# One transformer layer on one core: gate arithmetic over more half tiles, the norm before the FFN and the last 512 down columns by token tile, POOL's scale and shift behind the norm

## The chip, the core and the metric

The kernel runs on one core of a Trainium2 chip. The core has five engines that run at the same time and meet through semaphores: TensorE (PE) multiplies matrices, VectorE (DVE), ScalarE (ACT) and GpSimd (POOL) work element by element, SyncE (SP) starts transfers, which 16 DMA engines carry out. The metric is the device time of one execution in microseconds (us), the median of the runs; lower is better.

## The reference, cut to what matters

One layer over 256 tokens of 2048 features, all in float32. Every norm is over the 2048 features of a token.

```python
def _layer_norm(x, g, b):
    mu = mean(x, -1); var = mean(square(x - mu), -1)
    return (x - mu) * rsqrt(var + 1e-5) * g + b

def _conv_ffn(x, w_up, conv_w, conv_b, w_down):          # w_up 2048 x 11264, w_down 5632 x 2048
    gate, val = split(x @ w_up, 2, axis=-1)
    gate = _causal_dwconv(gate, conv_w, conv_b)          # 3 taps over the tokens
    return (gelu(gate) * val) @ w_down

x = _layer_norm(x, ln_in_g, ln_in_b)
x = _layer_norm(a * x + _hybrid_mixer(x, ...), ln1_g, ln1_b)                    # a = 2 ** 0.25
x = _layer_norm(a * x + _memory_cross_attention(x, mem, xq, xkv, xo), ln2_g, ln2_b)
x = _layer_norm(a * x + _conv_ffn(x, ffn_w_up, ...), ln3_g, ln3_b)              # the output
```

In the mixer, `_mlstm` takes a forget gate per head as `log_sigmoid(f_pre)`, sums it over the tokens, and keeps a running maximum of the input gate less that sum.

## The kernel before, in words

**Precision.** A float32 weight is cut in two parts that PE takes in its float32r format: `hi` (ACT casts it, L146) and `lo`, what is left (DVE subtracts, L147). Activations are cut the same way, into the two parts of a `parts` tile. A product is hi times hi, hi times lo and lo times hi: three matmuls.

**Weights.** `load_w` (L104) has SP fetch up to 1 MB of packed weights into one of three `raw` tiles (L112) and cuts it in two half tiles. Each half tile gets a `hi` and a `lo` buffer from `homes`: four buffers (`whl`), in the FFN three more (`whl2`). So ACT and DVE cut ahead of PE by as many half tiles as there are buffers.

**Two forms of product.** `cm_chunk` (L149) leaves channels on the partitions: 128 weight columns stand in PE, and the tokens move past, 512 columns where both parts move at once (L162), 256 for the first part against `lo` (L168). `tm_part` (L179) leaves tokens on the partitions: 128 tokens stand, and up to 512 weight columns move (L190), for both token tiles `tt` from one half tile. `tm_by_token` (L194) loads all half tiles first and then goes through token tile 0 and after it token tile 1 (L204). It is used for the last 256 of the 2048 columns of `xo` and of `down`.

**Order.** All engines take their instructions in order. The order on each engine is made when the program is built, by a scheduler that starts from the order of the code; `keep_in_program_order`, `issue_after` and the list `behind` (for the cuts of the coming half tiles) tie single instructions. Side work is written as a generator that `tick()` moves one `yield` forward after each half tile of the main stream.

**The gate job** (`gate_job`, L379). The twelve instructions of the log-sigmoid (L385 to L396) go on DVE, with an Exp and a Ln on ACT, in one piece. After one `yield` PE transposes the gates (L401, L402) and DVE makes the sums over the tokens (L406 to L410); four `yield`s later PE turns them back (L416).

**The norm before the FFN** (L744 to L758). After the last `xo` columns DVE adds the residual of a token tile (L648), takes its statistics (L652, L236), a few one-column instructions make the scale (`rsqrt`, L224 to L230, a Sqrt on ACT) and four instructions of 512 columns normalise it (L245). When both token tiles are through, `ln_transpose` takes blocks of 128 features: PE transposes (L254), ACT scales and shifts into `y` (L256), DVE rounds the first part (L258), and DVE or, for every second pair, POOL subtracts the second part (L259). Meanwhile `keep_warm(10)` gives PE ten matmuls whose results nobody reads (L84). `ln_affine` (L277) then lets POOL scale and shift `xt` itself for the residual, behind a small copy (`begun`).

**The FFN.** 44 chunks of `up` (each 128 gate and 128 value channels, L774) in four blocks of 11, and after each block the `down` columns (L789). In the last block the columns are 512, 512, 512, 256 and 256, the last by token (L786).

**The end.** Per token tile: residual and statistics of the last 256 columns, scale, then eight blocks of 128 tokens by 512 features: three by ACT and POOL (L806 to L808, `pooled`), five by DVE (L810, L811). Each goes out as 256 KB.

## Time and profile before

| | |
|---|---|
| median of 3 runs (lowest, highest) | 1542.41 us (1538.74, 1542.47) |
| the profiled execution: its own time, its span | 1544.83 us, 1542.8 us |
| PE, PEld busy | 98%, 85% of the span |
| DVE, ACT, POOL busy | 66%, 50%, 9% |
| mean granted clock of TensorE | 0.992 of full speed |
| moved by DMA | 292.87 MB, mean 190 GB/s |
| the chain of waits | PE 96%, DVE 2%, POOL 1%, ACT 1%, DMA 1% |

The span runs from the first to the last instruction; the execution's own time is 2.0 us longer. A row of the timeline gives the start, the length, the engine, the line of the kernel, the operation with its output and inputs, how many instructions were merged, and in brackets how long the engine sat idle before and what ended that. Matmuls overlap: how often one starts, not how long one lasts, tells what a stream of them costs. A plain float32 matmul leaves two records, a float32r matmul or a transpose one.

### The profile page before, as it was taken

The page shows a single profiled execution, that of the slowest core. Times are in us where ns is not written, and L with a number is a line of the kernel's source. Part 1 is how long each engine was busy: PE and PEld are TensorE (multiplying, and loading weights), DVE is VectorE, ACT ScalarE, POOL GpSimd, SP SyncE. Part 2 cuts the span into 40 slices and gives each one's busy share as a digit, 9 for nine tenths or more (in the row PEclk, how much of TensorE's full clock was granted, in tenths as well). Part 3 has the DMA queues.
Part 4 walks back from the last instruction along what each step waited for, and adds up shares of the span by engine and source line. Part 5 has one row for each costly group of instructions (what it writes and reads, how often), then busy time and mean ns, then how long its engine had stood idle before and what let it go on. Part 6 is the DMA issues. An engine that isn't in the chain of part 4 may idle for free.

```text
span 1542.8 us, 20558 instructions
## 1 busy us (share of the span) xinstructions
PE 1513.9 (98%) x8218; PEld 1318.0 (85%) x8218; DVE 1022.4 (66%) x1346; ACT 764.2 (50%) x987; POOL 142.6 (9%) x138
## 2 busy tenths in 40 slices
PE   8989999999999999999989999999999999999995
PEld 7988888888888888988878888888888888888885
DVE  6775999777776545664678765566655665566665
ACT  5554454586445445554355553455435554455541
POOL 1360000100006400000026000000000000000002
PEclk9999999999999999999999999999999999999998
DMA  9565555443655655444557555454554545545451
GB/s 344 173 210 194 189 196 179 171 174 134 255 204 198 219 191 191 141 152 151 192 189 240 198 198 203 177 207 169 203 202 171 212 168 198 207 168 215 160 195 55
DMA packets 46127, 292.87 MB, mean 190 GB/s; under 512 B 5392, under 2 KB 6032, under 8 KB 15312
## 3 DMA queue, kind: packets, MB, share of 16 engines
q1 hardware_dynamic: 43056, 282.64, 50.2%
q0 software_dynamic: 2544, 8.13, 2.6%
q8 instruction: 64, 1.05, 0.3%
q10 hardware_dynamic: 432, 0.79, 0.1%
q14 instruction: 31, 0.25, 0.0%
HBM read 289.44 MB, written 2.10 MB: 189 GB/s over the span
## 4 chain that ended last, share of the span: by engine, by line
PE 96%; DVE 2%; POOL 1%; ACT 1%; DMA 1%; SPq 0%; issue 0%; POOLq 0%; ACTq 0%
PE mm L190 37%; PE mm L162 35%; PE mm L168 19%; PE mm L204 1%; PE aux L693 1%; PE aux L723 1%; DMA raw<-wts_in 1%; POOL parts L259 1%; PE aux L254 0%; DVE xt L810 0%; ACT hi L146 0%; DVE lo L147 0%; PE aux L512 0%; PE aux L533 0%; ACT y L256 0%
## 5 line engine op out<-in xcount | busy, mean ns | idle before, releaser
L147 DVE TENSOR_TENSOR lo<-raw,hi 128x1024 fp32r<-128x1024 f32 (+4 forms) x536 | 645.5, 1226 | 358.9 <-ACT hi L146 280.0
L146 ACT CAST hi<-raw 128x1024 fp32r<-128x1024 f32 (+4 forms) x536 | 547.6, 1026 | 520.3 <-PE mm L190 270.4
L162 PE MATMUL mm<-parts,hi 128*128 128x512 f32 x2432 | 591.2, 393 | 2.7 <-POOL parts L259 2.7
L162 PEld LDWEIGHTS mm<-parts,hi 128*128 128x128 f32 x2432 | 446.8, 189 | 91.2 <-POOL parts L259 3.6
L168 PEld LDWEIGHTS mm<-parts,lo 128*128 128x128 f32 x2432 | 314.4, 191 | 13.6
L190 PE MATMUL mm<-hi,parts 128*128 128x512 f32 (+3 forms) x1088 | 318.0, 374 | 1.1 <-ACT hi L146 1.1
L168 PE MATMUL mm<-parts,lo 128*128 128x256 f32 x2432 | 318.8, 283 | 0.0
L190 PEld LDWEIGHTS mm<-hi,parts 128*128 128x128 f32 x1088 | 201.2, 190 | 34.5 <-ACT hi L146 2.0
L190 PE MATMUL mm<-hi,hp 128*128 128x512 f32 (+1 forms) x704 | 211.8, 382 | 0.0
L190 PE MATMUL mm<-lo,parts 128*128 128x512 f32 (+3 forms) x544 | 203.4, 374 | 1.2 <-DVE lo L147 1.2
L190 PEld LDWEIGHTS mm<-hi,hp 128*128 128x128 f32 x704 | 130.8, 188 | 25.7
L190 PE MATMUL mm<-lo,hp 128*128 128x512 f32 (+1 forms) x352 | 134.6, 383 | 0.0
L190 PEld LDWEIGHTS mm<-lo,parts 128*128 128x128 f32 x544 | 103.2, 190 | 18.3 <-DVE lo L147 2.6
L779 DVE SCALAR_TENSOR_TENSOR ac<-gv,pv,ac 128x255 f32<-128x255 f32 x88 | 50.1, 569 | 43.9 <-ACT ac L776 42.3
L172 ACT COPY gv<-mm 128x512 f32<-128x512 f32 x44 | 25.8, 586 | 103.9 <-PE mm L168 103.9
L190 PEld LDWEIGHTS mm<-lo,hp 128*128 128x128 f32 x352 | 66.2, 188 | 12.7
L807 POOL TENSOR_TENSOR xt<-xt,gb 128x512 f32<-128x512 f32 x3 | 4.5, 1496 | 677.5 <-ACT xt L806 677.5
L259 POOL TENSOR_TENSOR parts<-y,parts 128x512 fp32r<-128x512 f32 (+1 forms) x12 | 19.6, 1633 | 448.3 <-DVE parts L258 448.3
L451 DVE SCALAR_TENSOR_TENSOR cac<-cpad,pv,cac 128x256 f32<-128x256 f32 x120 | 51.3, 482 | 0.0
L287 POOL TENSOR_TENSOR xt<-xt,gb 128x512 f32<-128x512 f32 x24 | 41.6, 1752 | 43.6 <-DMA gb<-rows_in 36.6
L288 POOL TENSOR_TENSOR xt<-xt,gb 128x512 f32<-128x512 f32 x24 | 42.0, 1768 | 0.0
L781 DVE TENSOR_TENSOR ac<-gv,ac 128x256 f32<-128x256 f32 x44 | 19.2, 435 | 30.6 <-ACT ac L780 30.6
(227 smaller groups left out, 756.5 us busy)
## 6 DMA issues: line engine op xcount, KB each, us to landing
raw<-wts_in SPq DMA_DIRECT2D x238, 1024.0 KB, 4.9
raw<-wts_in SPq DMA_DIRECT2D x19, 768.0 KB, 4.3
gb<-rows_in POOLq DMA_DIRECT2D x24, 256.0 KB, 5.3
raw<-wts_in SPq DMA_DIRECT2D x4, 784.0 KB, 4.4
raw<-wts_in SPq DMA_DIRECT2D x6, 512.0 KB, 8.6
xt<-x_in SPq DMA_DIRECT2D x4, 512.0 KB, 9.7
raw<-memT_in SPq DMA_DIRECT2D x4, 512.0 KB, 3.6
gb<-rows_in SPq DMA_DIRECT2D x2, 1024.0 KB, 5.5
```

What stands on the lines that cost most here:

```text
L146: A.copy(hi, src)
L147: V.tensor_sub(lo, src, hi.bitcast(F32))
L162: nc.tensor.matmul(ps[:, j], lhsT=wH[:, kk, cs], rhs=a[:, k], start=(k == 0), stop=(k == KT - 1), skip_group_check=True)
L168: nc.tensor.matmul(ps[:, j, 0, :], lhsT=w[:, cs], rhs=a[:, k, 0, :], start=False, stop=(k == KT - 1), skip_group_check=True)
L172: A.copy(dst, ps[:, :, 1, :])
L190: nc.tensor.matmul(ps[tt][:, :n], lhsT=a[:, k, part, tsl], rhs=w[:, kk, :], start=(first and k == ks[0] and i == 0), stop=(last and k == k ...
L259: (G if k0 % 4 == 2 else V).tensor_sub(lo, y[:, 0:nk, :], hi.bitcast(F32))
L287: G.tensor_mul(sl, sl, gb[:, 0, :])
L288: G.tensor_add(sl, sl, gb[:, 1, :])
L451: tap = V.scalar_tensor_tensor(cac[:, i, :], cpad[:, i, j:j + S], pcol("ccw", i * CT + j), cac[:, i, :], ALU.mult, ALU.add)
L779: V.scalar_tensor_tensor(ac[:, o:], gv[:, 0, 0:S - o], pcol("fcw", f * 3 + t), ac[:, o:], ALU.mult, ALU.add)
L781: V.tensor_mul(ac, gv[:, 1, :], ac)
```

## The change

1. **Gates.** Seven `yield`s are put into the log-sigmoid's twelve instructions or behind them, and one between the sums over the tokens. The instructions are the same.
2. **Norm before the FFN.** The weights of the first `up` chunk are fetched and cut earlier, between the `xo` columns, into tiles of their own (`up0`, in the pool `pre`). `tm_by_token` calls `ln2_under` after each half tile, so the first token tile is normalised, transposed and cut (`ln_transpose_token`, four blocks of 128 features by 128 tokens at a time, always by DVE) beside the second token tile's matmuls. The first chunk is then multiplied by token tile (L829, L832 of the changed kernel): 64 matmuls of 2x128 columns and 64 of 128, where there were 32 of 512 and 32 of 256. `keep_warm` is gone. The second chunk's cuts are tied behind the norm's last ones, and POOL's copy `begun` reads the last part that the norm writes.
3. **Last down columns.** The last 512 columns (256 and 256) both go by token, the last 256 cut into a tile `wlast`. Each token tile is then closed whole: two residuals and statistics, scale, and all four blocks by DVE, written out by SP and ACT in turn. `pooled` is gone.

```diff
-    def load_w(mat, ks, cols):
+    def load_w(mat, ks, cols, into=None):
...
+            if into:
+                hi, lo = (t[:, k0 * n:k0 * n + sz] for t in into)
+            else:
...
+            after = behind.pop(0) if behind else []
...
+                with ExitStack() as order:
+                    for ins in after:
+                        order.enter_context(tc.issue_after(ins))
                     split(hi[:, o:e], lo[:, o:e], raw[:, k0 * n + o:k0 * n + e])
...
+    def cm_load(mat, c0, c1):
+        for g in range(0, KT, 8):
+            yield from load_w(mat, list(range(g, g + 8)), [(c0, c0 + P), (c1, c1 + P)])
...
+        for ks, wH, wL in loaded or cm_load(mat, c0, c1):
...
+        cm_close(ps, dst)
+    def cm_close(ps, dst, pinned=False):
+        copy = A.copy(dst, ps[:, :, 1, :])
+        if pinned:
+            tc.keep_in_program_order(copy)
...
-    def tm_by_token(a, mat, ks, cols, row0=0):
...
+    def tm_by_token(a, mat, ks, cols, row0=0, held=0, then=None):
+        store = act.tile([P, 2, 4096], F32R, name="wlast", tag="parts") if held else None
+        used, parts = 0, []
+        for c, col in enumerate(cols):
+            n = col[1] - col[0]
+            for g in range(0, len(ks), 8):
+                kg = [row0 + k for k in ks[g:g + 8]]
+                into = None
+                if c >= len(cols) - held:
+                    into = [store[:, i, used:used + len(kg) * n] for i in range(2)]
+                    used += len(kg) * n
+                parts += [(c, n, *p) for p in load_w(mat, kg, [col], into)]
+        ps = []
         for tt in range(NT):
-            for kl, wH, wL in parts:
+            ps.append(tm_open())
+            for pi, (c, n, kl, wH, wL) in enumerate(parts):
...
-                        nc.tensor.matmul(ps[tt][:, :n], lhsT=a[:, k, part, tt * P:(tt + 1) * P], rhs=w[:, kk, :],
+                        nc.tensor.matmul(ps[tt][c][:, :n], lhsT=a[:, k, part, tt * P:(tt + 1) * P], rhs=w[:, kk, :],
                                          start=(k == ks[0] and i == 0), stop=(k == ks[-1] and i == 2))
+                if then:
+                    then(ps, tt, pi)
         return ps
...
+    def ln_transpose_token(a, gname, bname, c, tt):
+        ps = aux.tile([P, 2, S], F32, name="aux").rearrange("p a (b t) -> p (a b) t", t=P)
+        y = yp.tile([P, 2, S], F32, name="y").rearrange("p a (b t) -> p (a b) t", t=P)
+        for k in range(4):
+            nc.tensor.transpose(ps[:, k, :], xt[:, tt, (4 * c + k) * P:(4 * c + k + 1) * P], ident)
+        for k in range(4):
+            made = A.activation(y[:, k, :], ps[:, k, :], AF.Identity, bias=pcol(bname, 4 * c + k), scale=pcol(gname, 4 * c + k))
+        hi, lo = (a[:, 4 * c:4 * c + 4, part, tt * P:(tt + 1) * P] for part in range(2))
+        V.tensor_copy(hi, y)
+        return made.ins, V.tensor_sub(lo, y, hi.bitcast(F32)).ins
...
-    def ln_affine(ri, rs):
-        tc.keep_in_program_order(G.tensor_copy(small.tile([P, NT], F32, name="begun"), rs))
+    def ln_affine(ri, begin):
+        tc.keep_in_program_order(G.tensor_copy(small.tile([P, NT], F32, name="begun"), begin))
...
             V.scalar_tensor_tensor(e, f, -1.0, f, ALU.mult, ALU.min)
+            yield
             A.activation(e, e, AF.Exp)
+            yield
             V.tensor_scalar_add(u, e, 1.0)
+            yield
             A.activation(w, u, AF.Ln)
             V.tensor_scalar_add(u, u, -1.0)
             V.tensor_scalar(z, u, 0.0, None, ALU.is_equal)
+            yield
             V.tensor_add(u, u, z)
             V.tensor_add(w, w, z)
+            yield
             V.reciprocal(u, u)
             V.tensor_mul(w, w, e)
+            yield
             V.tensor_mul(w, w, u)
             V.scalar_tensor_tensor(f, f, 0.0, w, ALU.min, ALU.subtract)
-            yield
+            for _ in range(3):
+                yield
...
             V.tensor_sub(g2, tg[0:4, 0:S], g1)
+            yield
             V.tensor_tensor_scan(mrow, g2, g2, 0.0, ALU.max, ALU.bypass)
...
-    for c in range(2, 4):
-        residual(tm_chunk(op, "xo", COLS_LAST[c]), c, COLS_LAST)
-    ps = tm_by_token(op, "xo", list(range(KT)), [COLS_LAST[4]])
-    xp = act_parts()
-    with keep_warm(10):
-        residual(ps, 4, COLS_LAST, tts=[0])
-        ln = ln_scales(len(COLS_LAST), [0])
-        for c in range(4):
-            ln_normalise(*ln, c, [0])
-        residual(ps, 4, COLS_LAST, tts=[1])
-        mv, rs = ln_scales(len(COLS_LAST), [1], ln)
-        for c in range(4):
-            norm = ln_normalise(mv, rs, c, [1])
-            first = norm if c == 0 else first
-            for k in range(4 * c, 4 * c + 4, 2 if c else 1):
-                ln_transpose(xp, "ln2_g", "ln2_b", k, 2 if c else 1)
-    ln_affine(4, rs)
+    with tc.tile_pool(name="pre", bufs=1) as pre:
+        up0 = [pre.tile([P, KT, 2 * P], F32R, name=n) for n in ("uph", "upl")]
+        for c in range(2, 4):
+            g = 8 * (c - 2)
+            into = [t[:, g:g + 8, :].rearrange("p k n -> p (k n)") for t in up0]
+            for _ in load_w("up", list(range(g, g + 8)), [(0, P), (DFF, DFF + P)], into):
+                pass
+            residual(tm_chunk(op, "xo", COLS_LAST[c]), c, COLS_LAST)
+        xp = act_parts()
+        ln, split0 = [], []
+        def ln2_norm(ps, tt):
+            with tc.issue_after(split0[1][1]) if tt else ExitStack():
+                residual([p[0] for p in ps], 4, COLS_LAST, tts=[tt])
+            ln.append(ln_scales(len(COLS_LAST), [tt], ln[-1] if ln else None))
+            for c in range(4):
+                ln_normalise(*ln[-1], c, [tt])
+        def ln2_under(ps, tt, pi):
+            if (tt, pi) == (0, 3):
+                ln2_norm(ps, 0)
+            if tt == 1 and pi >= 2:
+                for c in range(2 * pi - 4, 2 * pi - 2):
+                    split0.append(ln_transpose_token(xp, "ln2_g", "ln2_b", c, 0))
+        ps = tm_by_token(op, "xo", list(range(KT)), [COLS_LAST[4]], then=ln2_under)
+        ln2_norm(ps, 1)
+        ps0 = mm.tile([P, 2, 2, S], F32, name="mm")
+        for tt in range(NT):
+            tsl = slice(tt * P, (tt + 1) * P)
+            for g in range(0, KT, 4):
+                for i in range(2):
+                    for k in range(g, g + 4):
+                        for j in range(2):
+                            cs = slice(j * P, (j + 1) * P)
+                            if i == 0:
+                                nc.tensor.matmul(ps0[:, j, :, tsl], lhsT=up0[0][:, k, cs], rhs=xp[:, k, :, tsl], start=(k == 0),
+                                                 stop=(k == KT - 1), skip_group_check=True)
+                            else:
+                                nc.tensor.matmul(ps0[:, j, 0, tsl], lhsT=up0[1][:, k, cs], rhs=xp[:, k, 0, tsl], start=False,
+                                                 stop=(k == KT - 1), skip_group_check=True)
+                if tt == 0 and g >= 8:
+                    for c in range(g // 4 * 2 - 4, g // 4 * 2 - 2):
+                        split1 = ln_transpose_token(xp, "ln2_g", "ln2_b", c, 1)
+        behind.extend([[split0[3][0], split1[1]]] * 2 + [split1] * 2)
+        up1 = list(cm_load("up", P, DFF + P))
+    ln_affine(4, xp[:, KT - 1, 1, S - NT:S].bitcast(F32))
...
                 if f == 0:
-                    behind.extend([None] * 1 + [first.ins] * (4 - 1))
-                cm_chunk(xp, "up", f * P, DFF + f * P, gv)
+                    cm_close(ps0, gv, pinned=True)
+                else:
+                    cm_chunk(xp, "up", f * P, DFF + f * P, gv, up1 if f == 1 else None)
...
-            cols = COLS_LAST if final else COLS
-            for c in range(len(cols)):
...
+            if not final:
+                for c in range(4):
                     ps = tm_open()
-                    tm_part(ps, hp, "down", list(range(f1 - f0)), [cols[c]], row0=f0)
-                    residual(ps, c, cols, first=(bi == 0), last=final)
-    pooled = ((0, 0), (0, 1), (1, 0))
-    ln = None
-    nm = small.tile([P, NT], F32, name="nm")
+                    tm_part(ps, hp, "down", list(range(f1 - f0)), [COLS[c]], row0=f0)
+                    residual(ps, c, COLS, first=(bi == 0), last=False)
+            else:
+                for c in range(3):
+                    ps = tm_open()
+                    tm_part(ps, hp, "down", list(range(f1 - f0)), [COLS[c]], row0=f0)
+                    residual(ps, c, COLS_LAST, first=False)
+                last = tm_by_token(hp, "down", list(range(f1 - f0)), COLS_LAST[3:], row0=f0, held=1)
     for tt in range(NT):
-        residual(ps, 4, COLS_LAST, first=False, tts=[tt])
-        ln = ln_scales(len(COLS_LAST), [tt], ln)
-        mv, rs = ln
-        V.scalar_tensor_tensor(nm[:, tt:tt + 1], mv[:, tt, 0:1], -1.0, rs[:, tt:tt + 1], ALU.mult, ALU.mult)
-    for tt in range(NT):
+        for c in (3, 4):
+            n = COLS_LAST[c][1] - COLS_LAST[c][0]
+            sl = xt[:, tt, COLS_LAST[c][0]:COLS_LAST[c][1]]
+            tc.keep_in_program_order(V.tensor_add(sl, sl, last[tt][c - 3][:, 0:n]))
+            tc.keep_in_program_order(V.bn_stats(stats[:, tt, c, :], sl))
+        mv, rs = ln_scales(len(COLS_LAST), [tt])
         for c in range(4):
             cs = slice(c * 512, (c + 1) * 512)
             sl = xt[:, tt, cs]
-            if (tt, c) in pooled:
-                A.activation(sl, sl, AF.Identity, bias=nm[:, tt:tt + 1], scale=rs[:, tt:tt + 1])
-                G.tensor_mul(sl, sl, gb3[:, 0, cs])
-                G.tensor_add(sl, sl, gb3[:, 1, cs])
-            else:
-                V.scalar_tensor_tensor(sl, sl, mv[:, tt, 0:1], gb3[:, 0, cs], ALU.subtract, ALU.mult)
-                V.scalar_tensor_tensor(sl, sl, rs[:, tt:tt + 1], gb3[:, 1, cs], ALU.mult, ALU.add)
-                nc.sync.dma_start(out[tt * P:(tt + 1) * P, cs], sl)
-    for tt, c in pooled:
-        cs = slice(c * 512, (c + 1) * 512)
-        tc.keep_in_program_order(nc.scalar.dma_start(out[tt * P:(tt + 1) * P, cs], xt[:, tt, cs]))
+            tc.keep_in_program_order(V.scalar_tensor_tensor(sl, sl, mv[:, tt, 0:1], gb3[:, 0, cs], ALU.subtract, ALU.mult))
+            tc.keep_in_program_order(V.scalar_tensor_tensor(sl, sl, rs[:, tt:tt + 1], gb3[:, 1, cs], ALU.mult, ALU.add))
+            (nc.sync if c % 2 == 0 else nc.scalar).dma_start(out[tt * P:(tt + 1) * P, cs], sl)
```

Where instructions move, three places are shown, before and then changed.

PE at the gates, with token tiles of the gates `gm` transposed into `aux` between the matmuls of the value columns (`mm`). Before:

```order
L190 MATMUL mm<-lo,parts 128x384
L190 MATMUL mm<-hi,parts 128x384
L401 MATMUL aux<-ident,gm 128x128
L402 MATMUL aux<-ident,gm 128x128
L401 MATMUL aux<-ident,gm 128x128
L402 MATMUL aux<-ident,gm 128x128
L190 MATMUL mm<-hi,parts 128x384
L190 MATMUL mm<-lo,parts 128x384
```

Changed:

```order
L203 MATMUL mm<-lo,parts 128x256
L203 MATMUL mm<-hi,parts 128x256
L448 MATMUL aux<-ident,gm 128x128
L449 MATMUL aux<-ident,gm 128x128
L448 MATMUL aux<-ident,gm 128x128
L449 MATMUL aux<-ident,gm 128x128
L203 MATMUL mm<-hi,parts 128x256
L203 MATMUL mm<-lo,parts 128x256
```

The four transposes stand in the next group of columns now (256 wide, not 384): with 42 of 96 matmuls of the 384-wide group ahead of them before, and with all 96 of it and 72 of the next 96 now.

PE at the end of `xo` (`mm<-hi,parts`), the transposes of the norm (`aux<-ident,xt`) and the first `up` chunk (before `mm<-parts,hi`, now `uph` and `upl`). Before:

```order
L204 MATMUL mm<-hi,parts 128x256
L84 MATMUL aux<-ident 128x128 x10
L254 MATMUL aux<-ident,xt 128x128 x16
L162 MATMUL mm<-parts,hi 128x512 x3
L254 MATMUL aux<-ident,xt 128x128 x4
L162 MATMUL mm<-parts,hi 128x512 x4
L254 MATMUL aux<-ident,xt 128x128 x4
L162 MATMUL mm<-parts,hi 128x512 x2
L254 MATMUL aux<-ident,xt 128x128 x4
```

Changed:

```order
L230 MATMUL mm<-hi,parts 128x256
L294 MATMUL aux<-ident,xt 128x128 x8
L829 MATMUL mm<-parts,uph 128x2x128 x8
L832 MATMUL mm<-parts,upl 128x128 x8
L829 MATMUL mm<-parts,uph 128x2x128 x8
L832 MATMUL mm<-parts,upl 128x128 x8
L829 MATMUL mm<-parts,uph 128x2x128 x8
L832 MATMUL mm<-parts,upl 128x128 x8
L294 MATMUL aux<-ident,xt 128x128 x8
L829 MATMUL mm<-parts,uph 128x2x128 x8
```

The ten unread matmuls are gone. Eight transposes more stand 12 matmuls above the first row shown; the other 24 come in groups of eight, each group of the second token tile behind a part of the first tile's product.

DVE at the end, `xt` being the tokens, `mm` the last columns' sums. Before, from the middle of the first token tile's work:

```order
L811 SCALAR_TENSOR_TENSOR xt<-xt,rs,gb_6845 128x512
L650 TENSOR_TENSOR xt<-xt,mm 128x256
L811 SCALAR_TENSOR_TENSOR xt<-xt,rs,gb_6845 128x512
L652 BN_STATS stats<-xt 128x6
L236 BN_AGGR mv<-stats 128x2
L224 TENSOR_SCALAR ve<-mv 128x1
L810 SCALAR_TENSOR_TENSOR xt<-xt,mv,gb_6845 128x512
L226 RECIPROCAL rs<-nt 128x1
L810 SCALAR_TENSOR_TENSOR xt<-xt,mv,gb_6845 128x512
```

Changed, at the step from the first token tile to the second:

```order
L888 SCALAR_TENSOR_TENSOR xt<-xt,mv,gb_7009 128x512
L889 SCALAR_TENSOR_TENSOR xt<-xt,rs,gb_7009 128x512
L882 TENSOR_TENSOR xt<-xt,mm 128x256
L883 BN_STATS stats<-xt 128x6
L882 TENSOR_TENSOR xt<-xt,mm 128x256
L883 BN_STATS stats<-xt 128x6
L264 BN_AGGR mv<-stats 128x2
L252 TENSOR_SCALAR ve<-mv 128x1
L254 RECIPROCAL rs<-nt 128x1
```

Before, the two tiles' work is interleaved; now the second tile's residual stands behind all eight scalings of the first.

## Rows read from the trace of the kernel before

**Rows 1.** Waits of PE (who for whom: us in total, times, longest):
```profile
PE aux L401 <- DVE gm L396: 4.7, 1, 4.7
PE mm L162 <- POOL parts L259: 2.7, 2, 2.2
```

**Rows 2.** Timeline of PE at the gates (start us, us, engine, line, operation):
```profile
81.63 0.33 PE L190 MATMUL mm<-lo,parts 128*128 128x384 f32 x1
82.15 0.33 PE L190 MATMUL mm<-lo,parts 128*128 128x384 f32 x1
...
87.38 0.44 PE L401 MATMUL aux<-ident,gm 128*128 128x128 f32 x1 [4.72 <-DVE gm L396]
...
88.12 0.67 PE L190 MATMUL mm<-hi,parts 128*128 128x384 f32 x1
...
92.67 0.52 PE L190 MATMUL mm<-hi,parts 128*128 128x384 f32 x2
```

**Rows 3.** Windows at the gates: stretch, length, engines' busy (instructions), granted clock, DMA, GB/s:
```profile
88.10:92.70 4.60, 4.60 (x17) 4.60 (x16) 3.54 (x7) 0.83 (x1) 1.45 (x2) 0.52 0.54 114
```

**Rows 4.** Timeline of DVE at the gates:
```profile
87.07 0.17 DVE L396 SCALAR_TENSOR_TENSOR gm<-gm,gw 128x8 f32<-128x8 f32 x1
87.16 0.95 DVE L147 TENSOR_TENSOR lo<-raw,hi 128x768 fp32r<-128x768 f32 x1
```

**Rows 5.** Timeline of PE from the end of `xo` through three `up` chunks:
```profile
783.76 0.28 PE L204 MATMUL mm<-hi,parts 128*128 128x256 f32 x1
783.88 2.39 PE L84 MATMUL aux<-ident 128*128 128x128 f32 x20
...
794.81 0.73 PE L162 MATMUL mm<-parts,hi 128*128 128x512 f32 x2 [2.19 <-POOL parts L259]
...
819.46 7.44 PE L162 MATMUL mm<-parts,hi 128*128 128x512 f32 x32
826.74 4.00 PE L168 MATMUL mm<-parts,lo 128*128 128x256 f32 x32
830.57 1.78 PE L162 MATMUL mm<-parts,hi 128*128 128x512 f32 x7
```

**Rows 6.** Pieces of the chain of waits (start us, us, what):
```profile
97.72 0.98 PE aux L416 x8
...
772.52 10.09 PE mm L204 x84
```

**Rows 7.** Groups of instructions by line, shapes apart (count, busy us, mean ns):
```profile
L512 PE MATMUL aux<-qk 128*128 128x256 f32 x16 | 4.8, 380 | 0.0
L511 PE MATMUL aux<-qk 128*128 128x128 f32 x16 | 3.1, 275 | 0.0
L568 ACT ACTIVATE dm<-dm,atok 128x128 f32<-128x128 f32 x4 | 1.5, 386 | 0.0
L259 DVE TENSOR_TENSOR parts<-y,parts 128x512 fp32r<-128x512 f32 x11 | 7.6, 692 | 0.3
```

**Rows 8.** Timeline of DVE, first token tile of the norm before the FFN:
```profile
778.32 0.42 DVE L648 SCALAR_TENSOR_TENSOR xt<-xt,mm 128x256 f32<-128x256 f32 x1 [3.15 <-PE mm L204]
778.78 0.43 DVE L652 BATCH_NORM_STATS2 stats<-xt 128x6 f32<-128x256 f32 x1
...
780.87 1.92 DVE L245 TENSOR_SCALAR xt<-xt,mv,rs 128x512 f32<-128x512 f32 x4
```

**Rows 9.** Timeline of ACT in `xo`'s fourth group of columns:
```profile
766.80 1.05 ACT L146 CAST hi<-raw 128x1024 fp32r<-128x1024 f32 x1 [1.83 <-PE mm L190]
```

**Rows 10.** Timeline of the end, all engines:
```profile
1518.76 0.76 DVE L650 TENSOR_TENSOR xt<-xt,mm 128x256 f32<-128x256 f32 x2 [3.64 <-PE mm L190]
...
1524.04 1.40 DVE L810 SCALAR_TENSOR_TENSOR xt<-xt,mv,gb 128x512 f32<-128x512 f32 x2
...
1526.36 0.28 PE L204 MATMUL mm<-hi,hp 128*128 128x256 f32 x1
...
1537.53 1.59 POOL L808 TENSOR_TENSOR xt<-xt,gb 128x512 f32<-128x512 f32 x1
```

43 lines of the change are left out of this document (16 added, 27 removed).

## The prediction

> **What bounds the kernel now.** First the page's shares: PE is busy 98% of the span and makes up 96% of the chain of waits, so time is won where PE stands still or works without need, and nowhere else. The list of PE's waits comes next, and it is short: 4.7 us once for the gates on DVE, 2.7 us for POOL in the norm before the FFN [rows 1]. These waits are less than what the two places cost, because work around them is stretched too. So the third view is PE's timeline there: the reader is to compare the time between two points with what the same matmuls take elsewhere. The fourth place stands in no list of PE's waits, since PE has finished: from its last matmul at 1526.36 to the end of the span at 1542.8 are 16.4 us, in which DVE, ACT and POOL close the output [rows 10]. I treat the change as these three places and price each by its own rows.
>
> **Gates.** PE stands 4.72 us before the first transpose of the gates [rows 2]. After it PE runs at a granted clock of 0.52 on average, which is the 1.2 GHz level for nearly all of the stretch [rows 3]. That stretch holds 17 matmul records; two are the last transposes and one starts at its end, so 14 matmuls of 384 columns start between 88.12 and 92.67, 4.55 us. At the usual pace of 0.52 us for three [rows 2] they take 2.43 us: 2.1 us lost to the clock. The four transposes take 0.74 us from 87.38 to 88.12, where 0.12 each is usual (below): 0.3 us lost. Together 7.1 us.
>
> The new yields do not move DVE's arithmetic: in the built order its twelve instructions stay in one piece at the same place. What moves are the transposes, from behind 42 of this group's 96 matmuls to behind all of them and 72 of the next group's. PE so goes on past 82.5, and what is late next is the `lo` cut of the seventh half tile of 12 matmuls, which stands on DVE right behind the arithmetic and ends at 87.16 + 0.95 = 88.1 [rows 4]. PE reaches it after 6 matmuls of the fourth half tile and 24 of the next two, 30 x 0.173 = 5.2 us, at 87.7. I take 0.4 us for this wait, so 6.7 us won. With no wait of several microseconds the clock should not fall. ACT loads its table once more, for an Exp that comes between two Sigmoids, beside PE's work; DVE's sums over the tokens have more than two half tiles until PE asks for them.
>
> **Norm before the FFN.** From 783.88, where `xo` is done, two chunks of `up` and 32 transposes fill PE to 819.46: 35.6 us [rows 5]. One chunk in the steady run behind it takes from 819.46 to 830.57, 11.1 us [rows 5]. A 128x128 pass takes 0.12 us: the ten unread matmuls are 20 records in 2.39 us [rows 5]. So 2 x 11.1 + 32 x 0.117 = 26.0 us are needed and 9.6 us are lost: the unread matmuls, the waits, and the slow clock after them.
>
> The change starts the first token tile's norm 5.8 us earlier, beside the second tile's `xo` matmuls. Its price is PE work: the first chunk by token has 64 pairs of a matmul of 2x128 columns and one of 128. The 256-column matmuls of `xo` come every 0.12 us (84 in 10.09 us) [rows 6]; I take that for the 2x128 ones. A float32r matmul of 128 columns is not in the trace. From below, half of a 256-column one, 0.06 us, if the columns alone counted. From above, the plain float32 price: two passes of 0.117 for 128 columns, and for 256 columns two of 0.117 + 0.105 (380 less 275 ns [rows 7]), 0.44 us. The nearest row is the turning back of the gates: only four columns move, on 128 columns of weights, and one still comes every 0.98 / 8 = 0.12 us [rows 6], so the weights set the pace there. I take 0.12: 64 x 0.24 = 15.4 us, 4.3 more than the chunk before.
>
> The Trainium skill (TensorE: Matmul & The Clock Gate, "LDWEIGHTS") has a load take its columns over 1.2 per nanosecond, 107 ns for 128, whatever the rows; by that rule halving the columns of the moving side gains nothing, and the four-column row agrees. The same page ("Back-to-back issue gap") gives about 81 ns per matmul of 128 columns in a stream; the sum by that is an estimate of 5.2 us for the 64 narrow ones in place of 7.7, so 2.5 us more won, which no row here shows.
>
> Does the norm keep up? Count from 778.2, the first token tile's last matmul. DVE takes 2.55 us from the residual to the first normalised block and 0.48 per block [rows 8], so blocks stand at 3.1, 3.6, 4.1, 4.6. The first eight transposes stand 12 matmuls from the end, at 4.3: no wait. Each block of 128 features by 4 costs ACT 4 x 0.39 [rows 7] and DVE twice at most 0.69 [rows 7]: parts ready at about 7.5, 9, 10.5, 12. PE is through `xo` and its transposes at 7.6 and needs 1.9 us per quarter of a token tile's product, so the parts just keep ahead. DVE does the second tile's residual in between, from about 8.5, and normalises it by about 13 to 14.5; PE asks for it at 13.4. I take 0.5 us of waits in all. 9.6 - 4.3 - 0.5 = 4.8 us won. The earlier cut of the first chunk's weights (four more casts and subtractions in the `xo` columns) costs nothing as long as cutting waits for PE and not for the weights, as it does there [rows 9]; if it did not, four times 1.2 us on DVE would show. The second chunk's `lo` cuts wait behind the norm, but its first 32 matmuls, 7.3 us, need only `hi`. POOL starts some microseconds earlier than before, with the FFN's first residual far off.
>
> **The end.** A token tile's last matmul now comes after 66 instead of 33 of them. The first tile is complete where DVE begins the fourth group's residual today, 1518.76 [rows 10]. It takes one residual and statistics more (2 x 0.46), the same 2.55 us to the scale [rows 8], and eight scalings, 0.67 each where POOL is quiet (two end 1.40 after the first starts [rows 10]): 3.5 + 5.4 = 8.9, until 1527.6. PE's last matmul has ended by then (1526.6), so the second tile starts 1 us late and ends at 1536.5. Before, the last operation is POOL's, ending at 1539.12 [rows 10], 3.7 us ahead of the span's end, and what follows it is one output of 256 KB, as now. 2.6 us won. Cutting the last 256 columns into `wlast` waits for no buffer, so PE should not see it.
>
> **Sum.** 6.7 + 4.8 + 2.6 = 14.1 us, from 1544.8 us of the profiled execution to 1530.7. The median shown is 2.4 us below that execution, and so the forecast is 1542.4 - 14.1 = 1528.3, given as 1528.
>
> **Rivals.**
> *Narrow ones dear.* Only the 128-column matmuls cost the plain float32 price: 64 x (0.12 + 0.234) = 22.7, 11.6 more than before. 9.6 - 11.6 - 0.5 = -2.5 there, 6.8 in all: 1535.6. For it: plain float32 does pay two passes [rows 5]. Against: the operands stay float32r, and 256 columns of them run at a quarter of the plain price.
> *Both dear, and slower.* Moving the tokens in two pieces of 128 makes both kinds run at the plain price, PE being where it bites: 64 x (0.444 + 0.234) = 43.4, 32.3 more. 9.6 - 32.3 + 9.3 = -13.4: 1555.8. It decides from a pair at 0.47 us on, about twice what I take. Nothing in the trace speaks for it but that no row shows pieces.
> *The norm is late again.* ACT now has 32 instructions for 16, and the second tile's normalising stands behind the first's cuts on DVE; if each block came 1.2 us later, the 4.8 us go to waits, with a slow clock behind them: 1533.
> *The gates' wait only changes its name.* DVE's arithmetic is where it was, so if cuts behind it come as late as the transposes did, some 5 of 6.7 us stay: 1533.5. This is also the case in which the change does not do what it says. Against: PE has 30 matmuls ready that do not need the cuts.
> *Narrow ones cheap.* 0.06 us each saves 3.8 us on PE, of which the norm's pace gives back about 1: 1525.5.
>
> **How the numbers follow.** Forecast 0.52, narrow dear 0.14, both dear 0.07, norm late 0.13, gates 0.05, narrow cheap 0.09. The forecast's own range is 1524.5 to 1532, from the waits that I put at 0.4 to 1 us each. The range asked for goes from the cheap case to beyond the dear one: 1523 to 1538; outside it lie both dear and the tails of the others. What a measurement of this kernel can tell from no change is 0.3%, 4.6 us: faster is below 1537.8, slower above 1547. The dear, late and gates cases end mostly below it. Faster 0.86, same 0.07, slower 0.07.
>
> **What would show it.** Gates: no wait of PE at the transposes, a clock near 1 after them, and at most half a microsecond before the seventh half tile. Norm: the two matmuls of L829 and L832 both every 0.12 us, the second chunk done some 31 us after the last `xo` matmul, no wait for POOL. End: no POOL rows, the first token tile's scalings starting at about 3.5 us after its last matmul, and 13.5 to 14 us from the last matmul to the end. It is wrong if L832 costs over 0.2 us each, if PE waits for `lo` in the `xo` columns, or if the granted clock falls between the transposes.

## The result and the profile after

| | before | after |
|---|---|---|
| median (lowest to highest) | 1542.44 us (1538.74 to 1543.65) | 1530.07 us (1529.48 to 1530.86) |
| ratio after / before | | 0.9919, 95% interval 0.9906 to 0.9932 |
| the profiled execution: own time, span | 1544.83, 1542.8 us | 1529.72, 1527.8 us |
| PE busy, POOL busy | 98%, 9% | 99%, 9% |
| mean granted clock of TensorE | 0.992 | 0.996 |

The medians are 12.4 us apart, the profiled executions 15.1. The forecast was 1528 us: the time is 2 us longer, inside the range.

The list of PE's waits after (who for whom: us in total, times, longest) no longer has the two entries of [rows 1]:

```profile
PE aux L84 <- POOL ident L76: 1.6, 1, 1.6
PE mm L203 <- ACT hi L151: 1.4, 3, 0.8
PE mm L203 <- DVE lo L152: 1.4, 4, 0.8
PE mm L170 <- DVE gv L186: 0.3, 1, 0.3
```

What is left is the start of the program (up to 15.5 us), 0.16 us at the gates (below) and 0.3 us in the FFN.

**Gates.** The timeline of PE after, where [rows 2] had the wait of 4.72 us:

```profile
87.63 0.44 PE L203 MATMUL mm<-lo,parts 128*128 128x384 f32 x1 [0.16 <-DVE lo L152]
...
100.38 0.27 PE L448 MATMUL aux<-ident,gm 128*128 128x128 f32 x1
100.49 0.27 PE L449 MATMUL aux<-ident,gm 128*128 128x128 f32 x1
```

and the same window as in [rows 3] (the eighth field is the granted clock):

```profile
88.10:92.70 4.60, 4.60 (x31) 4.60 (x30) 4.36 (x4) 2.09 (x3) 2.33 (x2) 1.00 0.94 178
```

The transposes wait for nothing and come every 0.11 us, the clock is 1.00 where it was 0.52, and 31 matmul records lie in the window where 17 did, the last 8 of them with 256 columns in place of 384. DVE's arithmetic, in the timeline of DVE, stands where it stood [rows 4], still with 1.2 us for 8 elements:

```profile
82.26 1.26 DVE L432 TENSOR_SCALAR gu<-gu 128x8 f32<-128x8 f32 x1
83.55 1.22 DVE L433 TENSOR_SCALAR gz<-gu 128x8 f32<-128x8 f32 x1
84.81 1.21 DVE L435 TENSOR_TENSOR gu<-gu,gz 128x8 f32<-128x8 f32 x1
...
86.53 0.17 DVE L442 SCALAR_TENSOR_TENSOR gm<-gm,gw 128x8 f32<-128x8 f32 x1
```

**Norm.** The timeline of PE after, answering [rows 5], from the last transposes of the first token tile on:

```profile
777.11 1.04 PE L294 MATMUL aux<-ident,xt 128*128 128x128 f32 x8
778.19 1.21 PE L829 MATMUL mm<-parts,uph 128*128 128x256 f32 x8
779.24 1.00 PE L832 MATMUL mm<-parts,upl 128*128 128x128 f32 x8
780.08 1.16 PE L829 MATMUL mm<-parts,uph 128*128 128x256 f32 x8
...
794.86 7.50 PE L170 MATMUL mm<-parts,hi 128*128 128x512 f32 x32
802.20 4.00 PE L176 MATMUL mm<-parts,lo 128*128 128x256 f32 x32
806.03 1.30 PE L170 MATMUL mm<-parts,hi 128*128 128x512 f32 x5
```

Eight L832 start within 780.08 - 779.24 = 0.84 us, 0.105 each; eight of both take 1.83 to 1.89 us, 0.23 to 0.24 a pair. The second chunk is done 28.9 us after 777.11; eight transposes (1 us) already lie in front of that, so 29.9 us answer to the 35.6 of before.

**End.** The timeline of all engines after, answering [rows 10]:

```profile
1506.61 0.42 DVE L882 TENSOR_TENSOR xt<-xt,mm 128x256 f32<-128x256 f32 x1 [5.36 <-PE mm L230]
...
1509.82 0.74 DVE L888 SCALAR_TENSOR_TENSOR xt<-xt,mv,gb 128x512 f32<-128x512 f32 x1
...
1510.36 4.05 PE L230 MATMUL mm<-wlast,hp 128*128 128x256 f32 x33
...
1515.61 0.42 DVE L882 TENSOR_TENSOR xt<-xt,mm 128x256 f32<-128x256 f32 x1
...
1523.94 0.75 DVE L889 SCALAR_TENSOR_TENSOR xt<-xt,rs,gb 128x512 f32<-128x512 f32 x1
```

The scalings begin 3.2 us after the residual, and the second token tile starts 1.2 us after PE's last matmul ends (1514.4). That matmul starts at 1510.36 + 32 x 0.12 = 1514.2, so 13.6 us to the end of the span, where 16.4 were.

### The profile page after: what moved, and what is told of

Read it like the earlier page. It is cut to its first block, busy times and chain, and to the rows that moved or that the text cites. A ratio compares the mean times of both kernels' runs of the same rounds, so it can differ in the third digit from the quotient of the medians.

```text
span 1527.8 us, 20640 instructions
## 1 busy us (share of the span) xinstructions
PE 1509.6 (99%) x8262; PEld 1314.8 (86%) x8262; DVE 1022.2 (67%) x1350; ACT 764.2 (50%) x1001; POOL 131.3 (9%) x128
## 4 chain that ended last, share of the span: by engine, by line
PE 95%; DVE 3%; DMA 1%; ACT 1%; issue 0%; SPq 0%; POOL 0%; DVEq 0%; ACTq 0%
PE mm L170 36%; PE mm L203 35%; PE mm L176 18%; PE mm L230 1%; DMA raw<-wts_in 1%; DVE lo L152 1%; PE aux L741 1%; PE aux L771 1%; PE mm L829 1%; PE mm L832 0%; DVE xt L889 0%; DVE xt L888 0%; PE aux L282 0%; ACT hi L151 0%; PE aux L560 0%
## 5 line engine op out<-in xcount | busy, mean ns | idle before, releaser
L152 DVE TENSOR_TENSOR lo<-raw,hi 128x1024 fp32r<-128x1024 f32 (+3 forms) x528 | 639.7, 1235 | 336.2 <-ACT hi L151 260.8
L151 ACT CAST hi<-raw 128x1024 fp32r<-128x1024 f32 (+3 forms) x528 | 539.4, 1026 | 493.3 <-PE mm L203 250.9
L170 PE MATMUL mm<-parts,hi 128*128 128x512 f32 x2400 | 582.4, 393 | 0.3 <-DVE gv L186 0.3
L170 PEld LDWEIGHTS mm<-parts,hi 128*128 128x128 f32 x2400 | 440.6, 188 | 87.3 <-issue 0.7
L176 PE MATMUL mm<-parts,lo 128*128 128x256 f32 x2400 | 312.4, 282 | 0.0
L203 PE MATMUL mm<-hi,hp 128*128 128x512 f32 x660 | 205.9, 392 | 0.0
L203 PEld LDWEIGHTS mm<-hi,hp 128*128 128x128 f32 x660 | 124.1, 188 | 26.6
L203 PE MATMUL mm<-lo,hp 128*128 128x512 f32 x330 | 128.6, 390 | 0.0
L858 ACT ACTIVATE ac<-gv,pv 128x256 f32<-128x256 f32 x44 | 26.3, 599 | 26.8 <-DVE gv L186 26.8
L152 DVE TENSOR_TENSOR hp<-ac,hp 128x256 fp32r<-128x256 f32 x44 | 18.7, 426 | 21.5 <-ACT hp L151 21.5
```

Source lines behind the costliest of these rows:

```text
L151: A.copy(hi, src)
L152: V.tensor_sub(lo, src, hi.bitcast(F32))
L170: nc.tensor.matmul(ps[:, j], lhsT=wH[:, kk, cs], rhs=a[:, k], start=(k == 0), stop=(k == KT - 1), skip_group_check=True)
L176: nc.tensor.matmul(ps[:, j, 0, :], lhsT=w[:, cs], rhs=a[:, k, 0, :], start=False, stop=(k == KT - 1), skip_group_check=True)
L203: nc.tensor.matmul(ps[tt][:, :n], lhsT=a[:, k, part, tsl], rhs=w[:, kk, :], start=(first and k == ks[0] and i == 0), stop=(last and k == k ...
L858: A.activation(ac, gv[:, 0, :], AF.Identity, bias=pcol("fcb", f), scale=pcol("fcw", f * 3 + 2))
```

## The experiments

Each was timed against the kernel before in later rounds. "Changed" is the changed kernel with its 1530.07 us from above; e5, e10 and e11 build on one another. In the later rounds the kernel before has medians of 1543.55 to 1543.72 us, 1.1 to 1.3 above the 1542.44 of the result, and the changed kernel was not timed again. So the medians do not resolve a difference of about a microsecond to it.

| kernel | median (lowest to highest), us | ratio to before, interval |
|---|---|---|
| e1, gates back | 1537.00 (1535.31 to 1537.75) | 0.9961 (0.9947 to 0.9974) |
| e2, norm back | 1534.58 (1534.35 to 1534.91) | 0.9947 (0.9934 to 0.9959) |
| e3, end back | 1531.48 (1530.82 to 1532.38) | 0.9926 (0.9914 to 0.9939) |
| e4, narrow ones twice | 1537.89 (1537.45 to 1538.16) | 0.9967 (0.9955 to 0.9979) |
| e5, 64 bytes unused | 1528.55 (1528.02 to 1529.97) | 0.9902 (0.9887 to 0.9918) |
| e6, all at multiples of 128 | 1531.35 (1528.08 to 1532.31) | 0.9918 (0.9904 to 0.9932) |
| e7, gates back, fill | 1534.64 (1532.63 to 1534.86) | 0.9941 (0.9928 to 0.9953) |
| e8, chunk whole | 1534.27 (1533.79 to 1534.65) | 0.9940 (0.9928 to 0.9953) |
| e9, gates back, POOL later | 1529.61 (1529.12 to 1530.74) | 0.9911 (0.9894 to 0.9927) |
| e10, e5 and end early | 1528.86 (1528.23 to 1530.03) | 0.9908 (0.9893 to 0.9922) |
| e11, e10 and POOL later | 1527.29 (1526.09 to 1528.31) | 0.9896 (0.9882 to 0.9911) |
| e12, weight buffers back | 1532.07 (1529.91 to 1533.63) | 0.9925 (0.9912 to 0.9939) |

**One part undone (e1 to e3).** The hunks of the diff are taken back one at a time, as e1 does (it takes out eight `yield`s in or behind the log-sigmoid's instructions, for the change puts in eight there and not seven, and the one between the sums):

```diff
             A.activation(e, e, AF.Exp)
-            yield
             V.tensor_scalar_add(u, e, 1.0)
-            yield
...
-            for _ in range(3):
-                yield
+            yield
```

> The changed kernel with the gate job of the kernel before (no new yields); all else stays. Theory: the gates are worth what their place cost in the trace before, some 7 us (4.7 of waiting, 2.1 of slow clock, 0.3 of slow transposes), so 1530.1 + 7 = 1537 us, and PE again waits 4 to 5 us for DVE before the gate transposes, with a granted clock near 0.5 behind them. Rival: part of the gain only came from the neighbours (the cuts of the next half tiles late in either order): under 4 us slower, 1534 or less. Second rival: the gates explain the whole 7.6 us that the changed kernel is ahead at the last xo matmul of the first token tile, and a little more: 1538 or above.

> The changed kernel with the norm before the FFN and the first up chunk as they were before (both token tiles normalised, ten unread matmuls, 512 and 256 columns moving, POOL in the norm). Theory from the two traces: from the first token tile's last xo matmul to the end of the second up chunk 35.5 us where it was 41.3, so 5.8 us slower: 1535.9 us. Forecast's term: 4.8, so 1534.9. Rival: the FFN behind it, where the changed kernel took 692.5 us against 691.0, pays for the new order of buffers; then 1.5 us come back and the net is 4.3: 1534.4, with down groups of 512 columns again every 14.95 us rather than 15.1.

> The changed kernel with the last down columns and the output as they were before (512, 512, 512, 256, and only the last 256 by token tile; three blocks by ACT and POOL). Theory from the two traces: 16.4 us from PE's last matmul to the end in place of 13.5, so 2.9 us slower: 1533.0 us (forecast's term 2.6: 1532.7). Rival: taking the last 512 columns by token costs PE time that the tail hides in the comparison (cuts of 256 columns, a second buffer): then under 1.5 us slower.

Measured: 6.9, 4.5 and 1.4 us slower than changed, 12.8 in all, against 12.4 for the whole change: the parts add up. The spans of the profiled executions give 5.6, 4.9 and 1.8 us. e1 agrees with its theory. e2 agrees with the forecast's term; its rival has about the same size, but the rival's sign did not come (the down groups take 15.09 us, not 14.95). In e3 the rival's size came out, but not for the rival's reason. Its tail is as long as before (last matmul at 1513.19, span's end 1529.6: 16.4 us), so the new end is worth 2.8 us there. But PE comes to its last matmul 0.9 us earlier than in the changed kernel (there 1514.12), and the difference begins long before the end. The FFN's first residuals in e3, timeline of DVE:

```profile
921.58 1.29 DVE L696 SCALAR_TENSOR_TENSOR xt<-xt,mm 128x512 f32<-128x512 f32 x2
936.53 1.29 DVE L696 SCALAR_TENSOR_TENSOR xt<-xt,mm 128x512 f32<-128x512 f32 x2
```

and in the changed kernel, with the same order of instructions up to there:

```profile
921.75 1.29 DVE L696 SCALAR_TENSOR_TENSOR xt<-xt,mm 128x512 f32<-128x512 f32 x2
936.83 1.29 DVE L696 SCALAR_TENSOR_TENSOR xt<-xt,mm 128x512 f32<-128x512 f32 x2
```

A down group of 66 matmuls of 512 columns takes 14.95 us in one and 15.08 in the other. Before, too, it is 14.95; in e1, e2 and e4, with the new end, about 15.1.

**What 64 bytes do (e5, e6, e12).** The new end needs no tile `nm`. As the programs are built, `hp` and the FFN's own weight buffers so lie 64 bytes lower per partition: 96 above a multiple of 128, where they were 32 above one.

```diff
+    nc.vector.memset(small.tile([P, 8], F32, name="spare"), 0.0)     # e5 (two buffers: 64 bytes)
+    nc.vector.memset(const.tile([P, 24], F32, name="spare_c"), 0.0)  # e6, besides
+        ff1.tile([P, 16], F32, name="spare")                         # e12, alone
```

> The changed kernel with 64 bytes per partition left unused ahead of the FFN's tiles. Reason: the new end needs no nm tile, so hp and the three hi and lo buffers of the FFN lie 64 bytes lower than in the kernel before, and in all four kernels with the new end the down groups of 512 columns come every 15.1 us, in the two with the old end every 14.96, while up chunks are 0.2 % faster. Theory (the address): down groups every 14.96 us again, last PE matmul about 1 us earlier, 1529.2 us. Rival (something else in the new end, such as the tile wlast or its transfers): 15.1 us still, 1530.1.

> As the kernel with 64 bytes unused, and 96 more ahead of every large tile, so that the raw, hi, lo, parts and hp tiles all begin at a multiple of 128 bytes (before: 32 above one). If the place within 128 bytes sets the pace of the matmuls, up chunks and down groups change from 11.1 and 14.96 us by up to 1 % in either direction (1516 to 1542 us over the whole); if only the distance between hp and the weight buffers counts, which is the same as with 64 bytes, nothing changes against that kernel: 1529.2 us.

> The changed kernel with 64 bytes left unused between hp and the FFN's weight buffers: hp stays where the change put it (96 above a multiple of 128 bytes), the three hi and lo buffers of the FFN go back to 32 above one, as in the kernel before. If the place of the weight buffers sets the pace, down groups come every 14.96 us again as with 64 bytes ahead of both, 1529 us; if the place of hp does, 15.1 us as in the changed kernel, 1530.1 us; between the two, both count. Up chunks, which do not use hp, tell the weight buffers' part by themselves: 136.3 us between the fourth down group of a block and the first of the next where they lie as before, 136.06 as in the changed kernel.

In e5 the down groups come every 14.95 us again (timeline of DVE):

```profile
922.94 1.28 DVE L697 SCALAR_TENSOR_TENSOR xt<-xt,mm 128x512 f32<-128x512 f32 x2
937.89 1.28 DVE L697 SCALAR_TENSOR_TENSOR xt<-xt,mm 128x512 f32<-128x512 f32 x2
```

In e12, with `hp` where the change put it, every 15.10:

```profile
923.51 1.29 DVE L696 SCALAR_TENSOR_TENSOR xt<-xt,mm 128x512 f32<-128x512 f32 x2
938.61 1.28 DVE L696 SCALAR_TENSOR_TENSOR xt<-xt,mm 128x512 f32<-128x512 f32 x2
```

So the place of `hp`, which stands in PE in these matmuls, sets their pace. The weight buffers act on the up chunks, the other way. From a block's last down group to the next block's first there are eleven chunks and one down group. This takes 136.06, 136.28 and 136.12 us in the changed kernel, 136.34 each time in e5 and 136.49 in e12. The first of these stretches, timeline of DVE, in the changed kernel,

```profile
967.80 1.28 DVE L696 SCALAR_TENSOR_TENSOR xt<-xt,mm 128x512 f32<-128x512 f32 x2
...
1103.86 1.29 DVE L698 TENSOR_TENSOR xt<-xt,mm 128x512 f32<-128x512 f32 x2
```

and in e12:

```profile
969.61 1.28 DVE L696 SCALAR_TENSOR_TENSOR xt<-xt,mm 128x512 f32<-128x512 f32 x2
...
1106.10 1.29 DVE L698 TENSOR_TENSOR xt<-xt,mm 128x512 f32<-128x512 f32 x2
```

Less the down group, the eleven chunks take 121.0 to 121.2 us in the changed kernel and 121.4 in both others. e6 has 14.95 as well: `hp` at 0 or 32 above a multiple of 128 is fast, at 96 slow. Its distance to the FFN's own weight buffers is the same in the changed kernel as in e5, so that is not what counts; whether its place itself does or its distance to a tile that did not move, these kernels don't tell apart. In the trace e5 wins 0.8 us between its first down group and the last but one (561.14 us in place of 561.94); the medians say 1.5. The mechanism stays open, and `hp` put back with the weight buffers left low was not tried.

The medians of e6 and e12 miss their forecasts by 2 us, and the traces show where the profiled executions lose it. From the start of the second chunk to the first residual, the profiled executions take 126.9 us in the changed kernel, 128.3 in e5, 128.7 in e12 and 130.2 in e6. In that stretch PE's wait for `gv` goes from 0.3 us (changed) to 1.8 (e6), although each engine has the same instructions in the same order around it (790 to 860 us). There POOL scales and shifts for the FFN's residual, and a `lo` cut of 128x1024 takes DVE up to 2.3 us beside it, 1.22 later in the FFN; how many cuts are hit differs among the profiled executions. So the 64 bytes are to be read from the pace of the loops, not from medians a microsecond or two apart.

**The narrow matmul (e4).**

```diff
+                                for _ in range(2):
                                     nc.tensor.matmul(ps0[:, j, 0, tsl], lhsT=up0[1][:, k, cs], ...
```

> The changed kernel with each of the 64 matmuls of 128 columns of the first up chunk (weights upl) issued twice, so the lo product of that chunk is counted twice. Their price by itself. Theory: the load of the weights sets the pace, a little over 0.1 us each as the trace of the changed kernel has it (8 of them in 0.84 us), 64 x 0.105 = 6.7 us more where PE sets the pace there: 1536.8 us. If columns alone counted (0.06 us): 3.8 more, 1533.9. If they paid the plain float32 price (0.234): 15 more, 1545. If the norm and not PE set the pace in the first half of the chunk, up to half of it would vanish in waits: 1533.5 with waits of PE for DVE gone.

7.8 us slower, 0.12 for each of the 64; in the trace the second chunk starts 7.3 us later (802.17), 0.11 for each. The timeline of PE in e4:

```profile
779.64 1.90 PE L833 MATMUL mm<-parts,upl 128*128 128x128 f32 x16
781.38 1.15 PE L829 MATMUL mm<-parts,uph 128*128 128x256 f32 x8
```

16 in 1.74 us, 0.109 each: PE sets the pace, and half the columns save little. 0.06 and 0.234 are both excluded. The Trainium skill (TensorE: Matmul & The Clock Gate, "LDWEIGHTS") has 107 ns for loading 128 columns, which these rows bear out; the 81 ns of its "Back-to-back issue gap" no run here reaches.

**Token by token, or whole (e8).** The loop over `tt` around the first chunk is gone, and all transposes stand in front:

```diff
-        for tt in range(NT):
-            tsl = slice(tt * P, (tt + 1) * P)
+        for c in range(4):
+            split1 = ln_transpose_token(xp, "ln2_g", "ln2_b", c, 1)
```

> The changed kernel with the first token tile's norm as early as it is, but the first up chunk multiplied for both token tiles at once (32 matmuls of 512 columns and 32 of 256), behind all transposes. Theory: the split by token is what lets PE work under the second tile's norm; without it PE waits from the end of xo (777 us) until the second tile's first four blocks are cut (about 787), needs 11.1 us from there, plus 1 to 3 us of slow clock: the second chunk is done 4 to 7 us later, 1535 us. Rival: the split's 64 narrow matmuls cost more than they hide (4.3 us more PE time than the whole chunk): 1526 to 1529 us.

4.2 us slower. The timeline of PE in e8:

```profile
783.77 3.65 PE L294 MATMUL aux<-ident,xt 128*128 128x128 f32 x16 [5.85 <-DVE xt L273]
787.71 2.86 PE L829 MATMUL mm<-parts,uph 128*128 128x512 f32 x8 [0.29 <-DVE parts L299]
...
799.61 7.44 PE L170 MATMUL mm<-parts,hi 128*128 128x512 f32 x32
```

PE stands 5.85 us, and the second chunk starts at 799.61, not 794.86. The earlier norm alone is not enough: the split fills the wait.

**Why the gates were late (e7, e9).** e7 puts work into the wait; e9 moves POOL's scale and shift of the first norm behind the arithmetic.

```diff
+            fill = aux.tile([P, 512], F32, name="aux")                    # e7
+            for _ in range(18):
+                nc.tensor.matmul(fill[:, 0:P], lhsT=ident, rhs=ident, start=True, stop=True)
...
-        ln_affine(ri, rs)                                                 # e9, for the first norm
+            ln_affine(0, gm[:, 0, HM:HM + NT])                            # e9, behind the last gate arithmetic
```

> The changed kernel with the gate job of before, and 18 unread 128x128 float32 matmuls (4.2 us) put on PE ahead of the gate transposes, so that PE waits about as long in all but is busy in most of it; they also stand 6 matmuls earlier. Theory: the slow clock is the price of standing idle, so with the fill the granted clock behind the transposes is 1 and not 0.5, the 384-column matmuls go on at 0.52 us for three, and 2.1 to 2.4 us come back: 1537.0 - 2.3 = 1534.7 us. Rival: the clock falls all the same, or the slow stretch has another cause: 1537 us.

> The changed kernel with the gate job of before, and POOL's scale and shift of the first norm tied behind the gates' last arithmetic instead of in front of it; the order on PE and DVE stays. In the kernel before, L390 and L391 take DVE 1.18 us each for 8 elements, and POOL's 512-column operations run from 81.3 to 86.8 us, just then; where POOL is silent such an operation takes 0.17. Theory: POOL makes DVE's small operations wait, and that is most of the 4.7 us; with POOL later the arithmetic ends some 3.5 us sooner, PE waits about 1.2 us for the gates, and the slow clock behind it is shorter or gone: 1537.0 - 4 = 1533.0 us (1531.5 to 1533.5). Rival: the arithmetic's chain over DVE and ACT is as long by itself: a wait of 4 to 5 us again, 1537.

e7 came out at the forecast's time, yet it does not price the clock. Windows of e1, behind 4.7 us of standing idle (the eighth field is the granted clock),

```profile
86.50:88.00 1.50, 1.29 (x6) 1.32 (x7) 1.10 (x3) 0.00 (x0) 1.05 (x2) 0.50 0.12 36
88.00:90.00 2.00, 2.00 (x9) 2.00 (x8) 1.90 (x4) 0.26 (x1) 0.00 (x0) 0.64 0.67 145
```

and of e7, where PE was busy up to the transposes:

```profile
86.50:88.00 1.50, 1.50 (x10) 1.50 (x9) 1.47 (x2) 0.84 (x1) 1.50 (x2) 1.00 0.09 33
88.00:90.00 2.00, 2.00 (x13) 2.00 (x13) 1.90 (x2) 1.05 (x1) 1.70 (x3) 1.00 0.00 0
```

agree with the theory: the clock is 0.50 behind the idle stretch and 1.00 where there was none. But in e7 PE did not wait for DVE at all: nearly all of the arithmetic ran before POOL began (81.8 us). So part of the 2.4 us is shorter arithmetic, and the two were not separated.

e9 says where that comes from. Before, POOL's operations in the timeline of POOL,

```profile
81.33 3.04 POOL L287 TENSOR_TENSOR xt<-xt,gb 128x512 f32<-128x512 f32 x2 [3.47 <-DMA gb<-rows_in]
84.33 2.48 POOL L288 TENSOR_TENSOR xt<-xt,gb 128x512 f32<-128x512 f32 x2
```

lie over DVE's in its timeline:

```profile
83.21 1.18 DVE L390 TENSOR_SCALAR gz<-gu 128x8 f32<-128x8 f32 x1
84.43 1.18 DVE L391 TENSOR_TENSOR gu<-gu,gz 128x8 f32<-128x8 f32 x1
```

In e9 the same two, with POOL silent until 81.92:

```profile
80.72 0.17 DVE L431 TENSOR_SCALAR gz<-gu 128x8 f32<-128x8 f32 x1
80.93 0.17 DVE L432 TENSOR_TENSOR gu<-gu,gz 128x8 f32<-128x8 f32 x1
```

Not every operation on 8 elements is held up: L392 and L393, at 85.53 and 85.65, where one POOL operation gives way to the next, take 0.15 and 0.20 us before as well. PE's wait falls to 0.9 us (timeline of PE in e9), with a clock of 1.00 behind it:

```profile
81.92 0.30 PE L443 MATMUL aux<-ident,gm 128*128 128x128 f32 x1 [0.92 <-DVE gm L437]
```

The time falls from 1537.00 to 1529.61 us: 7.4 us, more than the 4 expected and as much as the spread gates give. The traces of e1 and e9 show 4.9 of them at the gates: 3.8 of waiting, 0.4 at the transposes, 0.8 of slow clock. (The profiled execution of e1 is its fastest and that of e9 its slowest.) Most of the wait of 4.7 us was POOL's doing. The Trainium skill (SBUF — State Buffer, "Who interferes with whom") has DVE operations with two SBUF inputs, and some with one, share a port pair with POOL, one of them blocked for the other's whole instruction; the 1.18 against 0.17 us agree.

**The end earlier, and both together (e10, e11).** Before 1506.61 DVE stands 5.36 us, since both halves of a token tile's columns lie in one PSUM tile. e10 gives each its own:

```diff
-            ps.append(tm_open())
+            ps.append([aux.tile([P, 512], F32, name="aux") for _ in cols] if held else tm_open())
```

> The kernel with 64 bytes unused, and the last 512 down columns accumulated in four PSUM tiles of one bank instead of two tiles of two, so that the first 256 columns of a token tile can be added while its last 256 are multiplied. In the changed kernel DVE stands idle for 5.4 us before that residual and is then busy to the end. Theory: the end is DVE's work, so one residual with statistics (0.85 us) done earlier brings the end 0.85 us nearer: 1528.55 - 0.85 = 1527.7 us, 12.6 us from the last matmul to the end of the span in place of 13.5. Rival: the add waits for the last of the token tile's matmuls all the same, or disturbs them: 1528.5 or more.

> The kernel with four PSUM tiles at the end and 64 bytes unused, and POOL's first scale and shift behind the gates as well, with the spread gates of the change. Theory: the spread gates already leave no wait there, so POOL's place is worth nothing more: 1527.7 us. Rival: POOL beside the first cuts also costs DVE time that PE feels (the 1.4 us that PE waits for lo, in four places); then up to 1 us less: 1526.7.

The first add now runs under the tile's last matmuls, timeline of DVE in e10:

```profile
1503.06 0.42 DVE L883 TENSOR_TENSOR xt<-xt,aux 128x256 f32<-128x256 f32 x1 [1.47 <-PE aux L231]
...
1507.02 0.42 DVE L883 TENSOR_TENSOR xt<-xt,aux 128x256 f32<-128x256 f32 x1 [3.08 <-PE aux L231]
...
1523.57 0.75 DVE L890 SCALAR_TENSOR_TENSOR xt<-xt,rs,gb 128x512 f32<-128x512 f32 x1
```

The span ends 0.7 us earlier than in e5 with the FFN at the same place (first residual 923.00 and 922.94); the medians, 1528.86 and 1528.55, do not resolve it. e11 is 1.6 us faster than e10, more than its rival's 1.0, and the traces place the difference. Between 15 and 88 us e11 wins 0.7 us on e10, where PE's wait for `lo` of 0.43 us at 87.23 is gone: that is the rival's effect. The larger part lies in the FFN, at the collision described with e12. In e10 three of four cuts on DVE run into POOL's scale and shift of the norm before the FFN, and PE waits for `gv`:

```profile
821.26 7.92 DVE L153 TENSOR_TENSOR lo<-raw,hi 128x1024 fp32r<-128x1024 f32 x4
829.84 7.55 PE L171 MATMUL mm<-parts,hi 128*128 128x512 f32 x32 [1.61 <-DVE gv L187]
```

In e11 two of the four do, and PE does not wait:

```profile
819.85 6.83 DVE L153 TENSOR_TENSOR lo<-raw,hi 128x1024 fp32r<-128x1024 f32 x4
827.89 7.44 PE L171 MATMUL mm<-parts,hi 128*128 128x512 f32 x32
```

Each engine has the same order of instructions in both there, so it is not shown that POOL's place at the gates brings this part; moving POOL's work before the FFN was not tried. At 1527.29 us e11 beats both kernels, and its slowest execution is below the fastest of the changed kernel.

## Why the prediction was right, and where it was off

1. **Gates: 6.7 won; measured 6.9 (e1).** Each sign held: arithmetic unmoved, no wait at the transposes, a clock of 1.00, and a short wait for the seventh half tile's `lo` (0.16 us where 0.4 were put). The size was right within what these runs resolve: the profiled executions give 5.6, as the slow clock of e1's ends at about 89.2 us (0.96 on average from there to 92.0) and that of before at 92.7. The account stopped short: "DVE's arithmetic" was taken as given, while most of its length was DVE held up by POOL (in e9 the wait of 4.7 us shrank to 0.9). The rows with 1.18 us for 8 elements were there to be read.
2. **Norm: 4.8 won; measured 4.5 (e2).** In the trace, to the end of the second chunk, 35.6 - 29.9 = 5.7 us: the narrow matmuls cost 0.105 to 0.109, a little under the 0.12 taken from the four-column row. Both dear rivals fell, and so did the cheap one (e4). Of the 0.5 us of waits some 0.4 are to be seen (before 778.19 and before the transposes at 783.97). About 0.6 us came back in the chunks behind, 0.3 of it PE's wait for `gv`. The sign "some 31 us after the last `xo` matmul" was 28.9, since eight transposes lie inside `xo` and the narrow matmuls cost a little less.
3. **End: 2.6 won; measured 1.4 (e3), 1.8 between the profiled executions.** This is the term that was mis-sized. The tail itself gave 2.8 (13.6 us against 16.4), as its steps had it: 3.2 us to the scalings, the second tile 1.2 us late. What the sum left out is that taking `nm` away moves `hp` and the FFN's weight buffers by 64 bytes. In the 561.94 us of the changed kernel named above, the ten steps from one down group of a block to the next lose 1.3 us in all against e5, and the three stretches with the up chunks win 0.6: the FFN pays 0.8 us, and PE's last matmul comes 0.9 us later than in e3.
4. **Sum: 14.1; measured 12.4.** The interval of the ratio leaves 10.5 to 14.5 us. The profiled executions differ by 15.1 mainly because that of before lay 2.4 us above its median, which the forecast took into account. With the 64 bytes put back (e5) the time is 1528.55, at the forecast; e6, with the same pace in the FFN, has 1531.35, so this closeness is in part luck.
5. **The rivals.** The gates' wait did not change its name, the norm was not late, nothing ended on the slower side.

## What to carry to other kernels

Where an operation on a few elements takes a microsecond, look at what another engine does in the same moments before spreading or hiding it: moving POOL's work (e9) gave as much as spreading the gates. A tensor engine that would wait for a norm can be given half the tokens, even at twice the instructions, where the added work is less than the wait: here some 3.7 us more for the 64 pairs of narrow matmuls, against 5.85 us of standing still in e8. When a change drops or adds a small tile, compare the pace of untouched loops in both traces: the tiles laid out behind it have moved.

## What the runs showed of the hardware

- A 64-byte move of the stationary operand of 512-column float32r matmuls changes their pace by 1% (14.95 to 15.10 us for 66), and of the FFN's weight buffers that of the `up` chunks by 0.2 to 0.3% in the other direction (121.4 to 121.0 or 121.2 us for eleven); no wait shows it.
- Some DVE operations on 8 elements take 1.18 us beside POOL's 512-column operations and 0.17 without them; a float32 subtraction of 128x1024 takes up to 2.3 us in place of 1.22.
- A float32r matmul of 128 columns comes every 0.105 to 0.109 us, one of 256 every 0.12.
